# Hybrid GLA/NSA/SSD decoder trunk: the mixers' small TensorE products regrouped by array tile shape

## The chip, the core and the metric

The kernel runs on one core of one Trainium2 chip. The metric is the device time of one execution in microseconds, as the median of several runs. [...] In what follows the tile shape is written rows x columns, so 64x128 is half of the rows and all columns.

## The reference

Two layers on 256 tokens of 1,024 features, float32. In each layer an RMSNorm and one input projection feed three token mixers. Their outputs are concatenated, projected and added to the residual, and an MLP with squared ReLU follows.

```python
for l in range(DEPTH):
    u = rms_norm(h, norm1_w[l])
    proj = u @ w_in[l]
    ...
    y_gla = gla_mixer(...)
    y_nsa = nsa_mixer(...)
    y_ssd = ssd_mixer(...)
    h = h + jnp.concatenate([y_gla, y_nsa, y_ssd], axis=-1) @ w_out[l]
    u = rms_norm(h, norm2_w[l])
    h = h + jnp.square(jax.nn.relu(u @ w_up[l])) @ w_down[l]
return rms_norm(h, final_norm_w)
```

- **GLA** (gated linear attention, 4 heads of 32 keys and 64 values): a gate of rank 16 gives a log decay per key, summed along the tokens (B). Attention between tokens i and j is weighted by exp(B_i - B_j).
- **NSA** (sparse attention, 4 heads of 64, two per key/value group g): each query attends to 15 compressed keys, to selected blocks and to a window, with a softmax for each of the three branches; with 256 tokens the selected blocks and the window are all earlier tokens. The compressed keys and values come from a small MLP (2,048 to 128 to 64) over blocks of 32 tokens.
- **SSD** (Mamba-2, 8 heads of 64, state 128): a causal convolution, a cumulative decay per head, chunked scan in two chunks of 128 tokens, gated norm.

## The kernel before

Tokens are two halves t of 128. Weights come in pieces of 512 KB: `load_w` (L172) issues the DMA on SyncE's queue into one of three raw buffers, `split_w` (L181) makes a high part (a cast, mostly on ScalarE, L100) and a low part (a subtraction on VectorE, L189) in five buffers each, and a matrix product is then three TensorE passes (`mm3`, L262, and L428 to L430). So the large products are float32r of shape 128x128. The mixers' small products are plain float32, each of which appears as two TensorE instructions, and transposes.

The work of a layer's first part is written as five generators (L400 to L988): `s_proj` (13 units of 256 columns of the input projection, order in `CFG['porder']`), `s_nsa`, `s_gla`, `s_ssd` and `s_out`. `drive` (L272) steps the one whose own clock is lowest, each `yield` being a cost, and so sets the order in which instructions are written; the scheduler of the framework then places each ready instruction by that order. Engines execute in the order that comes out of this at build time. While a mixer waits for VectorE or ScalarE, TensorE thus has projection matmuls to do. Small products write to a pool of four PSUM banks (`psb`, L107), projections to another four (`psa`).

The small products that matter here, with the tile shape that they use:

- `s_gla`: transposes of the gate's 16 columns (L797), the gate product with 16 rows (L800: 32x128). Then three levels of block products. Level 0 (L881) has stationary operands of 32, 64 and 96 columns; levels 1 and 2 (L899) are 32x32-token blocks, 24 products of 32 columns for each level and token half (128x32), and the diagonal products (L923) eight more for each half. Each level's factors (VectorE, ScalarE) are written just ahead of its products, the diagonal ones after level 2. The output product `goT` (L936 128x128 for t=1, L939 128x64) is written for t=0 before the diagonal products of t=1.
- `s_ssd`: five products for the cumulative decays `aps` (L664 to L667), three of them with 8 or 16 stationary columns, alternating with two of 128; two DMAs (L673, L674) move the negated sums to four partitions, and a copy and a subtraction make `acs_st` (L680, L681).
- `s_nsa`: the second product of the compression MLP (L518 with 64 columns per group, L521 with 15). For each token half and each head (r, g) `score` (L550) writes a mask into a bank by a bf16 product with the identity (L557, 128x128), adds the scores by a product with 64 rows (L560 for t=0; L563, L565 for t=1: 64x128, g choosing the lower or the upper half of the rows), for t=1 adds a second mask (L566, 128x128), and then takes three maxima (VectorE, L569) and three exponentials (ScalarE, L571). `trans` (L574) transposes the probabilities, and `value` (L594) multiplies: one product with the 15 compressed values (L601: 15 rows, 32x128) and two or four of 128 rows (L604). `NSEQ` (L29) is the order of these steps.

```python
PE.matmul(sa[:, :271], lhsT=identb, rhs=mask_t1 if t else mask_t0, start=True, stop=False)
...
PE.matmul(sa[:, :271], lhsT=q1, rhs=kT[gs, 0:271], start=False, stop=True)
sb = psb(f"sb{l}{t}{hh}")
PE.matmul(sb[:, :256], lhsT=q1, rhs=kT[gs, 271:527], start=True, stop=False)
PE.matmul(sb[:, 128:256], lhsT=identb, rhs=mask_cau, start=False, stop=True)
```

The compression MLP's first weights (`w1`, L498) use the same three raw buffers as the projection's weights, and hold two of them until its products (L501) have run.

Of the kernel before, what the change touches and what calls it, by code (L numbers as in the profile page):

```python
# [7 lines left out]
F32 = mybir.dt.float32  # L8
# [20 lines left out]
NSEQ = ([("s", 0, 0), ("s", 0, 1), ("t", 0, 0), ("s", 1, 0), ("t", 0, 1), ("s", 1, 1), ("v", 0), ("t", 1, 0), ("t", 1, 1), ("v", 1)],  # L29
        [("s", 0, 0), ("s", 0, 1), ("t", 0, 0), ("s", 1, 0), ("t", 0, 1), ("s", 1, 1), ("c",), ("t", 1, 0), ("v", 0),  # L30
# [16 lines left out]
for _n, _w in (("ident", 128), ("tri", 128), ("sfx", 128), ("ones64", 128), ("sel", 128), ("hmask", 4),  # L47
               ("sel4", 30), ("cosk", 128), ("sink", 128), ("cosq", 128), ("sinq", 128), ("valid", 2), ("e", 8), ("ta", 2)):
    _cf(_n, _w)
# [3 lines left out]
for _n, _w in (("n1", 8), ("n2", 8), ("gb", 1), ("gn", 2), ("nn", 2), ("cw", 32), ("cb", 8), ("sn", 4),  # L53
               ("pos", 32), ("w2", 128), ("dtb", 8), ("alog", 8), ("dsk", 8)):
    PF[_n] = (PF_N, PF_N + _w)
    PF_N += _w
# [3 lines left out]
def trunk(ctx, tc, x, w_in, w_out, w_up, w_down, w1, par, gate2, fnw, constf, constb, consti, out):  # L60
# [22 lines left out]
    rp = ctx.enter_context(tc.tile_pool(name="rp", bufs=2))  # L83
# [31 lines left out]
    with prio(-20000):  # L115
# [3 lines left out]
        for l in range(L):  # L119
            p = mpool.tile([128, PF_N], F32, name=f"par{l}", tag="par", bufs=2)  # L120
            g2 = mpool.tile([16, 128], F32, name=f"g2_{l}", tag="g2", bufs=2)
            pars.append(p)
            gates2.append(g2)
# [6 lines left out]
    with prio(5):  # L130
# [3 lines left out]
        SP.dma_start(gates2[0], gate2[0])  # L134
# [7 lines left out]
    mask_t1 = cb[:, 399:670]  # L142
    mask_ssd = cb[:, 670:798]
    mask_cau = cb[:, 128:256]
    hmask = C("hmask")
    sel = C("sel").rearrange("p (r m) -> p r m", r=2)
    cosk, sink, cosq, sinq = (C(n).rearrange("p (t d) -> p t d", t=2) for n in ("cosk", "sink", "cosq", "sinq"))
# [3 lines left out]
    onesc = cpool.tile([128, 128], F32, name="onesc")  # L151
    V.memset(onesc, 1.0)
    with prio(-30000):
        wps = psb("warm")
        for _ in range(CFG["warm"]):
            PE.matmul(wps[:, 0:128], lhsT=onesc, rhs=onesc, start=True, stop=True)
# [13 lines left out]
    G.memset(zt, 0.0)  # L170

# [125 lines left out]
    for l in range(L):  # L297
        p, g2 = pars[l], gates2[l]
        if l:
            SP.dma_start(p, par[l])  # L300
            SP.dma_start(g2, gate2[l])
# [19 lines left out]
        misc = mpool.tile([128, 2, 36], F32, name=f"misc{l}", tag="misc")  # L321
# [27 lines left out]
        def ev1(t, ps):  # L349
            rope(q_r[:, t], ps, 4, cosq, sinq, t, f"q{l}{t}")  # L350
# [103 lines left out]
        def s_nsa():  # L454
            w2 = P_["w2"].rearrange("p (v d) -> p v d", v=2)
# [8 lines left out]
            cp("qT", qT, qps.rearrange("p (r t) -> p r t", r=2), "A")  # L464
# [25 lines left out]
            gl = mpool.tile([128, 2, 30], F32, name=f"gl{l}", tag="gl")  # L490
            vc = mpool.tile([15, 128], F32, name=f"vc{l}", tag="vc")

            def comp(kv):
# [21 lines left out]
                V.tensor_tensor(gl[:, kv], t1, xx, OP.mult)  # L515
                for g in range(2):
                    if kv == 0:
                        PE.matmul(cps[g * 64:g * 64 + 64, 320:335], lhsT=w2[:, 0], rhs=gl[:, 0, g * 15:g * 15 + 15],  # L518
                                  start=True, stop=True)
                    else:  # L520
                        PE.matmul(cps[0:15, 336 + g * 64:400 + g * 64], lhsT=gl[:, 1, g * 15:g * 15 + 15], rhs=w2[:, 1],  # L521
                                  start=True, stop=True)
                if kv == 0:
                    A.copy(kT[:, 256:271], cps[:, 320:335])
                else:
                    A.copy(vc, cps[0:15, 336:464])
# [16 lines left out]
            br = (1, 0, 2)  # L543
            for t in range(2):
                segs = [(0, 128), (128, 143), (143, 271)] if t == 0 else [(0, 256), (256, 271), (271, 527)]
                sm = [spool.tile([128, 2, 3], F32, name=f"sm{l}{t}{r}", tag="sm", bufs=4) for r in range(2)]
                prs, pts, pcs = {}, {}, []
                yn = n2(f"yn{l}{t}", [128, 2, 128])

                def score(r, g):  # L550
                    gs = slice(g * 64, g * 64 + 64)
                    hh = 2 * g + r
                    pr = prp.tile([128, 527], F32, name=f"pr{l}{t}{hh}", tag="pr")
                    prs[r, g] = pr
                    q1 = qT[gs, r, t * 128:t * 128 + 128]
                    sa = psb(f"sa{l}{t}{hh}")
                    PE.matmul(sa[:, :271], lhsT=identb, rhs=mask_t1 if t else mask_t0, start=True, stop=False)  # L557
                    nm = spool.tile([128, 3], F32, name=f"nm{l}{t}{hh}", tag="nm", bufs=4)
                    if t == 0:
                        PE.matmul(sa[:, :271], lhsT=q1, rhs=kT[gs, 128:399], start=False, stop=True)  # L560
                        src = [sa[:, a:b] for a, b in segs]
                    else:
                        PE.matmul(sa[:, :271], lhsT=q1, rhs=kT[gs, 0:271], start=False, stop=True)  # L563
                        sb = psb(f"sb{l}{t}{hh}")
                        PE.matmul(sb[:, :256], lhsT=q1, rhs=kT[gs, 271:527], start=True, stop=False)  # L565
                        PE.matmul(sb[:, 128:256], lhsT=identb, rhs=mask_cau, start=False, stop=True)  # L566
                        src = [sa[:, 0:256], sa[:, 256:271], sb[:, 0:256]]
                    for i in range(3):
# [626 lines left out]
```

## Time and profile before

| | us |
|---|---|
| median of 3 runs | 699.27 (699.01 to 699.5) |
| the profiled execution, first to last instruction | 698.9 |
| TensorE busy | 678.2 |
| VectorE busy | 473.7 |
| ScalarE busy | 367.7 |
| mixers and projections of layer 0, of layer 1 | about 10 to 172, 350 to 510 |
| MLP of layer 0, of layer 1 | about 172 to 349, 510 to 686 |

A row of the timeline view has the start of the first instruction of a run of equal ones, the time until the last of them ends, the engine, line, operation, output and inputs, the stationary operand's shape (rows*columns), the moving one's, and how many there are. [...] A row of the windows view has, for one stretch, its length, then each engine's busy time and instructions, the granted TensorE clock as a share, the busy share of the DMA engines and GB/s.

### The profile page before, as it was taken

The page shows a single profiled execution, that of the slowest core. Times are in us where ns is not written, and L with a number is a line of the kernel's source. Part 1 is how long each engine was busy: PE and PEld are TensorE (multiplying, and loading weights), DVE is VectorE, ACT ScalarE, POOL GpSimd, SP SyncE. Part 2 cuts the span into 40 slices and gives each one's busy share as a digit, 9 for nine tenths or more (in the row PEclk, how much of TensorE's full clock was granted, in tenths as well). Part 3 has the DMA queues.
Part 4 walks back from the last instruction along what each step waited for, and adds up shares of the span by engine and source line. Part 5 has one row for each costly group of instructions (what it writes and reads, how often), then busy time and mean ns, then how long its engine had stood idle before and what let it go on. Part 6 is the DMA issues. An engine that isn't in the chain of part 4 may idle for free.

```text
span 698.9 us, 12400 instructions
## 1 busy us (share of the span) xinstructions
PE 678.2 (97%) x4926; PEld 607.8 (87%) x4926; DVE 473.7 (68%) x880; ACT 367.7 (53%) x704; POOL 5.5 (1%) x16
## 2 busy tenths in 40 slices
PE   4999999999999999999999999999999999999996
PEld 4987888987999898989898889798889999999995
DVE  5885886988755555554579878788886555555535
ACT  7344856656644444454364376764575444444433
POOL 2000000000000000000000000000000000000000
PEclk9998999999999999999999999999999999999999
DMA  8524741433765555556414374332466655555521
GB/s 276 188 80 154 225 121 58 121 117 126 238 212 187 188 191 188 181 182 187 153 61 152 113 235 142 96 119 84 129 205 213 207 183 187 189 192 184 181 91 60
DMA packets 31873, 111.81 MB, mean 160 GB/s; under 512 B 3688, under 2 KB 4296, under 8 KB 31816
## 3 DMA queue, kind: packets, MB, share of 16 engines
q1 hardware_dynamic: 31816, 111.04, 49.2%
q8 instruction: 38, 0.62, 0.3%
q14 instruction: 19, 0.16, 0.1%
HBM read 109.94 MB, written 1.05 MB: 159 GB/s over the span
## 4 chain that ended last, share of the span: by engine, by line
PE 90%; DMA 4%; DVE 3%; ACT 2%; issue 0%; SPq 0%; DVEq 0%; ACTq 0%
PE acc L263 8%; PE up L264 8%; PE up L265 8%; PE up L263 8%; PE acc L265 8%; PE acc L264 8%; DMA r_in<-in_w_in 4%; PE pj L263 3%; PE pj L265 3%; PE pj L264 3%; PE pj L428 3%; PE pj L429 3%; PE pj L430 3%; PE op L265 2%; PE op L263 2%; PE op L264 2%
## 5 line engine op out<-in xcount | busy, mean ns | idle before, releaser
L265 PE MATMUL up<-xh_b,l_u 128*128 128x256 f32 x480 | 135.7, 283 | 0.0
L264 PE MATMUL up<-xl_b,h_u 128*128 128x256 f32 x480 | 135.7, 283 | 0.0
L263 PE MATMUL up<-xh_b,h_u 128*128 128x256 f32 x480 | 135.7, 283 | 0.0
L189 DVE TENSOR_TENSOR l_d<-r_d,h_d 128x1024 fp32r<-128x1024 f32 x64 | 78.4, 1225 | 70.2 <-ACT h_d L100 69.9
L189 DVE TENSOR_TENSOR l_u<-r_u,h_u 128x1024 fp32r<-128x1024 f32 x64 | 78.2, 1224 | 69.1 <-ACT h_u L100 69.0
L100 ACT CAST h_u<-r_u 128x1024 fp32r<-128x1024 f32 x64 | 67.1, 1049 | 82.8 <-PE up L264 40.1
L100 ACT CAST h_d<-r_d 128x1024 fp32r<-128x1024 f32 x64 | 67.0, 1048 | 80.3 <-PE up L264 43.7
L265 PE MATMUL acc<-h_d,ul 128*128 128x512 f32 (+1 forms) x288 | 106.7, 370 | 0.0
L264 PE MATMUL acc<-l_d,uh 128*128 128x512 f32 (+1 forms) x288 | 106.3, 369 | 0.0
L263 PE MATMUL acc<-h_d,uh 128*128 128x512 f32 (+1 forms) x288 | 106.2, 369 | 0.0
L264 PEld LDWEIGHTS up<-xl_b,h_u 128*128 128x128 f32 x480 | 91.9, 191 | 0.6
L263 PEld LDWEIGHTS up<-xh_b,h_u 128*128 128x128 f32 x480 | 91.8, 191 | 0.6
L265 PEld LDWEIGHTS up<-xh_b,l_u 128*128 128x128 f32 x480 | 91.9, 192 | 0.0
L189 DVE TENSOR_TENSOR l_in<-r_in,h_in 128x1024 fp32r<-128x1024 f32 (+2 forms) x54 | 64.3, 1194 | 20.1 <-ACT h_in L100 19.7
L100 ACT CAST h_in<-r_in 128x1024 fp32r<-128x1024 f32 (+2 forms) x50 | 50.9, 1021 | 36.9 <-PE pj L265 10.6
L263 PE MATMUL pj<-h_in,xh_a 128*128 128x256 f32 (+1 forms) x224 | 66.2, 296 | 0.0
L265 PE MATMUL pj<-h_in,xl_a 128*128 128x256 f32 (+1 forms) x224 | 65.8, 295 | 0.0
L264 PE MATMUL pj<-l_in,xh_a 128*128 128x256 f32 (+1 forms) x224 | 65.0, 291 | 0.0
L263 PEld LDWEIGHTS acc<-h_d,uh 128*128 128x128 f32 x288 | 54.3, 189 | 9.8 <-ACT uh L231 0.8
L265 PEld LDWEIGHTS acc<-h_d,ul 128*128 128x128 f32 x288 | 54.1, 188 | 10.0 <-DVE ul L232 0.4
L264 PEld LDWEIGHTS acc<-l_d,uh 128*128 128x128 f32 x288 | 54.1, 188 | 9.4
L428 PE MATMUL pj<-xh_a,h_in 128*128 128x256 f32 x192 | 57.2, 298 | 2.0 <-ACT h_in L100 2.0
(347 smaller groups left out, 1244.7 us busy)
## 6 DMA issues: line engine op xcount, KB each, us to landing
r_u<-in_w_up SPq DMA_DIRECT2D x64, 512.0 KB, 3.3
r_d<-in_w_down SPq DMA_DIRECT2D x64, 512.0 KB, 3.3
r_in<-in_w_in SPq DMA_DIRECT2D x48, 512.0 KB, 4.3
r_o<-in_w_out SPq DMA_DIRECT2D x16, 512.0 KB, 3.5
r_w<-in_w SPq DMA_DIRECT2D x8, 512.0 KB, 4.3
r_in<-in_w_in SPq DMA_DIRECT2D x4, 438.0 KB, 3.7
out_dram<-o SPq DMA_DIRECT2D x4, 256.0 KB, 2.0
r_in<-in_w_in SPq DMA_DIRECT2D x2, 292.0 KB, 3.9
```

Source lines behind the costliest of these rows:

```text
L100: A.copy(dst, src)
L189: i_ = V.tensor_tensor(lo[:, :n], raw[:, :n], hi[:, :n].bitcast(F32), OP.subtract)
L263: PE.matmul(ps, lhsT=lh, rhs=rh, start=start, stop=False)
L264: PE.matmul(ps, lhsT=lh, rhs=rl, start=False, stop=False)
L265: PE.matmul(ps, lhsT=ll, rhs=rh, start=False, stop=stop)
L428: PE.matmul(o, lhsT=wh[:, ts], rhs=xh[:, k], start=k == 0, stop=False)
L429: PE.matmul(o, lhsT=wh[:, ts], rhs=xl[:, k], start=False, stop=False)
L430: PE.matmul(o, lhsT=wl[:, ts], rhs=xh[:, k], start=False, stop=k == 7)
```

## The change

No large product changes. The mixers' small products do:

- **Scores in pairs.** `score(r, part)` now does both groups g at once: two masks first (128x128), then the product of g=0 on the lower row half and that of g=1 on the upper, into two PSUM banks, then the maxima and exponentials of both. For t=1 the two parts of the row are separate steps; the second part's mask is now 256 columns wide and stands first. A scheduling order (`behind`) keeps the products behind both masks. `NSEQ` has the new order.
- **Padding with zeros to 128x128.** The 15 compressed values and probabilities (`vc`, `pc`, `pt`), the gate's operands (`misc`, `g2`, `glT`), the decay increments (`dap`: one product of 128 columns gives the sums of both halves on partitions 0 to 7 and 32 to 39, in place of three narrow ones), the compression's second product (`glp`, `w2` with its key half twice) and GLA's level 0. The padded tiles are cleared by GpSimd once at the start.
- **GLA levels in a row.** The factors of levels 1 and 2 and of the diagonal are written one after the other; then, for each token half, all small products of levels 1, 2 and the diagonal follow each other, and then their copies. Both `goT` come after that, with the 128x128 products ahead of the 128x64 ones.
- **What follows from these:** four DMAs in place of two for the negated sums, two copies and two subtractions for `acs_st`, the copy of the compressed keys in two parts (ScalarE and VectorE), the query scale of 1/8 in the copy of `qT` instead of in two tables (256 constant columns fewer), one rope buffer in place of two.

```diff
-NSEQ = ([("s", 0, 0), ("s", 0, 1), ("t", 0, 0), ("s", 1, 0), ("t", 0, 1), ("s", 1, 1), ("v", 0), ("t", 1, 0), ("t", 1, 1), ("v", 1)],
-        [("s", 0, 0), ("s", 0, 1), ("t", 0, 0), ("s", 1, 0), ("t", 0, 1), ("s", 1, 1), ("c",), ("t", 1, 0), ("v", 0),
+NSEQ = ([("s", 0, 0), ("s", 1, 0), ("t", 0, 0), ("t", 0, 1), ("v", 0), ("t", 1, 0), ("t", 1, 1), ("v", 1)],
+        [("s", 0, 0), ("s", 0, 1), ("s", 1, 0), ("t", 0, 0), ("s", 1, 1), ("t", 0, 1), ("c",), ("t", 1, 0), ("v", 0),
...
+                    for g in range(2):
+                        mk = mask_w1 if part else mask_t1 if t else mask_t0
+                        i_m = PE.matmul(sc[g][:, 0:n], lhsT=identb, rhs=mk, start=True, stop=False)
+                    for g in range(2):
+                        i_s = PE.matmul(sc[g][:, 0:n], lhsT=q1[g], rhs=kT[g * 64:g * 64 + 64, k0:k0 + n], start=False, stop=True)
+                        if g == 0:
+                            behind(i_s, i_m)
...
-                        pcx = pt[0:15, 256:384] if t == 0 else pcs[0][:, (r * 2 + g) * 128:(r * 2 + g) * 128 + 128]
+                        pcx = pt[:, 256:384] if t == 0 else pcs[0][:, (r * 2 + g) * 128:(r * 2 + g) * 128 + 128]
...
-            for t in range(2):
-                if t:
-                    PE.matmul(aps[:, 8:16], lhsT=C("tri"), rhs=da[:, t], start=True, stop=True)
-                PE.matmul(aps[0:8, 128 + t * 128:256 + t * 128], lhsT=da[:, t], rhs=C("tri"), start=True, stop=True)
+            PE.matmul(aps[:, 8:16], lhsT=C("tri"), rhs=da[:, 1], start=True, stop=True)
             PE.matmul(aps[:, 16:24], lhsT=C("sfx"), rhs=da[:, 0], start=True, stop=True)
-            PE.matmul(aps[0:16, 384:512], lhsT=da.rearrange("p t h -> p (t h)"), rhs=C("tri"), start=True, stop=True)
+            PE.matmul(aps[:, 128:256], lhsT=dap.rearrange("p a b -> p (a b)"), rhs=C("tri"), start=True, stop=True)
...
-            SP.dma_start(nst[0:2], nah.bitcast(F32))
-            SP.dma_start(nst[2:4], nal.bitcast(F32))
+            for t in range(2):
+                SP.dma_start(nst[t:t + 1], nah[32 * t:32 * t + 8].bitcast(F32))
+                SP.dma_start(nst[2 + t:3 + t], nal[32 * t:32 * t + 8].bitcast(F32))
...
+            factors(0)
+            yield 3.0
+            for t in range(2):
+                ps = psb(f"gl{l}{t}0")
+                for a in (1, 2, 3):
+                    PE.matmul(ps[:, (a - 1) * 128:a * 128].rearrange("p (h s) -> p h s", h=4),
+                              lhsT=kv_lv[0][:, a - 1, t * 128:t * 128 + 128],
+                              rhs=qls[0].rearrange("p h (n a s) -> p h n a s", n=2, a=3)[:, :, t, a - 1],
+                              start=True, stop=True)
...
+            factors(1)
+            yield 3.0
+            factors(2)
...
+            for t in range(2):
+                gp = psb(f"gl{l}{t}x")
+                for i in (1, 2):
...
+                            PE.matmul(gp[32 * b:32 * b + 32, o:o + 32].rearrange("p (h n s) -> p h n s", h=4, n=w),
+                                      lhsT=kv_lv[i][:, a - 1, t * 128 + 32 * b:t * 128 + 32 * b + 32], rhs=rhs,
+                                      start=True, stop=True)
                 for z in range(2):
                     for b in range(4):
                         c0 = t * 128 + 32 * b
-                        PE.matmul(gps[t][32 * b:32 * b + 32, 192 + z * 64:256 + z * 64].rearrange("p (h n) -> p h n", h=4),
+                        PE.matmul(gp[32 * b:32 * b + 32, 192 + z * 64:256 + z * 64].rearrange("p (h n) -> p h n", h=4),
                                   lhsT=(k4 if z else ks)[:, c0:c0 + 32], rhs=qbd[:, :, c0 + z:c0 + 32:2],
                                   start=True, stop=True)
...
+                if t == 1:
+                    for pr_ in range(2):
+                        PE.matmul(goT[:, pr_ * 128:pr_ * 128 + 128], lhsT=gst[:, pr_ * 128:pr_ * 128 + 128], rhs=qx,
+                                  start=pr_ == 0, stop=False)
+                for hh in range(4):
+                    z, pr_ = hh % 2, hh // 2
+                    PE.matmul(goT[z * 64:z * 64 + 64, pr_ * 128:pr_ * 128 + 128], lhsT=gv[:, t, hh * 64:hh * 64 + 64],
+                              rhs=at[:, hh], start=t == 0, stop=t == 0 or hh >= 2)
```

More of the change, by code (lines that the diff above doesn't have):

```diff
@@ L150, in trunk @@
     mask4 = ci[:, 24:56].rearrange("p (z n) -> p z n", z=2)
-    onesc = cpool.tile([128, 128], F32, name="onesc")
+    onesc = cpool.tile([128, 1], F32, name="onesc")
     V.memset(onesc, 1.0)
[L153 to L156, printed above, removed]
     er = cpool.tile([68, 8, 128], FR, name="er")
@@ L514, in comp @@
                 V.reciprocal(t1, t1)
[L515 to L518, printed above, removed]
-                                  start=True, stop=True)
[L520 to L526, printed above, removed]
+                V.tensor_tensor(gl[:, kv * 30:kv * 30 + 30], t1, xx, OP.mult)
+                if kv == 0:
+                    PE.matmul(cps[:, 320:350], lhsT=w2[:, 0:128], rhs=gl[:, 0:30], start=True, stop=True)
+                    A.copy(kT[0:64, 256:271], cps[0:64, 320:335])
+                    V.tensor_copy(kT[64:128, 256:271], cps[64:128, 335:350])
+                else:
+                    for g in range(2):
+                        PE.matmul(cps[:, 352 + g * 64:416 + g * 64], lhsT=gl[:, 30 + g * 15:g * 15 + 158], rhs=w2[:, 128:192],
+                                  start=True, stop=True)
+                    A.copy(vc[0:15], cps[0:15, 352:480])
                 yield 2.0
@@ L542, in s_nsa @@
                 yield None
-            br = (1, 0, 2)
             for t in range(2):
-                segs = [(0, 128), (128, 143), (143, 271)] if t == 0 else [(0, 256), (256, 271), (271, 527)]
                 sm = [spool.tile([128, 2, 3], F32, name=f"sm{l}{t}{r}", tag="sm", bufs=4) for r in range(2)]
-                prs, pts, pcs = {}, {}, []
+                prs, nms, pts, pcs = {}, {}, {}, []
                 yn = n2(f"yn{l}{t}", [128, 2, 128])
[L550 to L561, printed above, removed]
-                    else:
[L563 to L568, printed above, removed]
-                        V.tensor_reduce(nm[:, br[i]:br[i] + 1], src[i], AX.X, OP.max, negate=True)
-                    for i, (a, b) in enumerate(segs):
-                        A.activation(pr[:, a:b], src[i], AF.Exp, bias=nm[:, br[i]:br[i] + 1],
-                                     accum_out=sm[r][:, g, br[i]:br[i] + 1])
@@ L679, in s_ssd @@
             A.activation(edc, aps[:, 16:24], AF.Exp)
-            A.copy(acs_st[0:8, :], aps[0:8, 128:384])
-            V.tensor_tensor(acs_st[32:40, :], aps[0:8, 128:384], acs_st[0:8, :].bitcast(F32), OP.subtract)
             yield 1.0
```

200 lines of the change are left out of this document (106 added, 94 removed).

## The prediction

> **What bounds the kernel now.** I read the page first, for who is busy and who holds the end.
>
> ```profile
> span 698.9 us, 12400 instructions
> PE 678.2 (97%) x4926; PEld 607.8 (87%) x4926; DVE 473.7 (68%) x880; ACT 367.7 (53%) x704; POOL 5.5 (1%) x16
> PE 90%; DMA 4%; DVE 3%; ACT 2%; issue 0%; SPq 0%; DVEq 0%; ACTq 0%
> ```
>
> TensorE is busy nearly all the time and is 90% of the chain that ended last. So a microsecond of TensorE's time counts, unless it lies in one of the few stretches in which TensorE waits for another. "Busy" here also holds what a product loses at its borders, and that shows in the timeline of TensorE: look at the distance of the starts, not at the durations.
>
> ```profile
> 32.55 0.28 PE L428 MATMUL pj<-xh_a,h_in 128*128 128x256 f32 x1
> 32.67 0.28 PE L429 MATMUL pj<-xl_a,h_in 128*128 128x256 f32 x1
> ...
> 34.47 0.38 PE L430 MATMUL pj<-xh_a,l_in 128*128 128x256 f32 x1
> 34.70 0.28 PE L428 MATMUL pj<-xh_a,h_in 128*128 128x256 f32 x1
> ```
>
> ```profile
> 137.63 1.00 PE L749 MATMUL yp<-xdt,mt 128*128 128x64 f32 x8
> 138.47 0.38 PE L738 MATMUL seg<-cb 128*128 128x512 bf16 x1
> ```
>
> Projection matmuls follow each other every 0.12 us (32.55, 32.67), each with its own weights; small float32 products of the full shape every 0.105 (0.84 for eight). But after the ten `aps` instructions of changing shape the first projection matmul takes 0.23 until the next starts (34.47, 34.70). The rule that I read from this and from the rows below: when the tile shape changes, the instruction ahead of the border costs about 0.09 us more, since the array has to run empty, and the first one behind it some 0.10 more, since the next weights can't be loaded under it (less for fewer stationary columns). A border thus costs up to 0.19 us, and the change is about borders.
>
> **Part 1: values (L601 padded from 15 to 128 rows).**
>
> ```profile
> 86.26 0.28 PE L557 MATMUL sa<-cb 128*128 128x271 bf16 x1
> 86.47 0.72 PE L560 MATMUL sa<-kT,qT 64*128 64x271 f32 x2
> 87.12 0.43 PE L601 MATMUL no<-vc,pt 15*128 15x64 f32 x2
> 87.48 0.66 PE L604 MATMUL no<-vsw,pt 128*128 128x64 f32 x4
> 88.06 0.43 PE L601 MATMUL no<-vc,pt 15*128 15x64 f32 x2
> ```
>
> ```profile
> L601 PE MATMUL no<-vc,pt 15*128 15x64 f32 x16 | 3.4, 294 | 0.0
> L601 PE MATMUL no<-vc,pc 15*128 15x64 f32 x16 | 3.4, 294 | 0.0
> ```
>
> From 87.12 to 88.06 six instructions take 0.94 us; without borders six take 0.66 at 0.11. That is 0.28 a product. The 32 instructions in the two groups are 16 products, 8 in a layer: 2.24 us per layer. The padding adds nothing on TensorE, since 64 moving columns on a full set of weights cost the 0.11 anyway; the copy of `pc` has as many elements per partition as before.
>
> **Part 2: scores in pairs.** For t=0 mask and score take 0.86 us (86.26 to 87.12), and the follower pays 0.10: 0.96, four times, 3.84 us. A pair afterwards: mask 0.12, mask ahead of the border 0.21 (86.26 to 86.47), first product 0.33, last 0.32 (the 0.65 from 86.47 to 87.12), 0.10 behind: 1.08 us, if the two row halves work at the same time. If they work one after the other, two more instructions of 0.23 (0.32 less the 0.09): 1.54. Two pairs: saved 1.68, or 0.76. For t=1:
>
> ```profile
> 101.11 0.28 PE L557 MATMUL sa<-cb 128*128 128x271 bf16 x1
> ...
> 102.48 0.28 PE L557 MATMUL sa<-cb 128*128 128x271 bf16 x1
> ```
>
> 1.37 us each, four times 5.48. Afterwards each r has two pairs, 1.08 and about 1.04 with 256 in place of 271 columns: 4.24 for two r, saved 1.24; one after the other 6.1, so 0.6 lost. The row halves at the same time are not in this trace. The nearest rows are column tiles:
>
> ```profile
> 49.14 1.11 PE L501 MATMUL cps<-r_w,zt 128*32 128x128 f32 x32
> 50.07 0.33 PE L899 MATMUL gl00x<-ql,klv 128*32 128x32 f32 x18
> ```
>
> 32 instructions in 0.93 us: eight rounds of about 0.11, each with four column tiles at once. I take the row halves as doing the same: 2.92 us per layer, with 0.2 as the other end. [...] No run here shows it yet.
>
> **Part 3: decays, gate, level 0.** `aps`: 2.03 us from 32.67 to 34.70. Afterwards three products, six instructions at 0.11, between two projection matmuls of 0.12: 0.90. Saved 1.13.
>
> ```profile
> 30.26 0.28 PE L428 MATMUL pj<-xh_a,h_in 128*128 128x256 f32 x1
> ...
> 31.37 0.28 PE L430 MATMUL pj<-xh_a,l_in 128*128 128x256 f32 x1
> ```
>
> ```profile
> 40.52 0.28 PE L264 MATMUL pj<-l_in,xh_a 128*128 128x256 f32 x1
> 40.73 2.25 PE L881 MATMUL gl<-ql,klv 128*32 128x128 f32 x12
> ...
> 42.93 0.28 PE L263 MATMUL pj<-h_in,xh_a 128*128 128x256 f32 x1
> ```
>
> The gate product with its neighbours takes 1.11; without borders two projection matmuls (0.24) and two of 256 columns (0.44): saved 0.43. Level 0: 2.41 from 40.52 to 42.93; afterwards 12 x 0.11 and two of 0.12, 1.56: saved 0.85. Together 2.4 us per layer. But they stand in a stretch where VectorE is nearly full:
>
> ```profile
> 27.00:44.00 17.00, 17.00 (x126) 14.49 (x125) 15.45 (x45) 8.71 (x29) 0.00 (x0) 1.00 0.42 138
> 50.30:57.40 7.10, 5.54 (x139) 4.60 (x125) 4.67 (x27) 2.76 (x8) 0.00 (x0) 0.99 0.49 150
> 57.40:64.10 6.70, 6.69 (x58) 5.48 (x59) 3.37 (x11) 0.95 (x3) 0.00 (x0) 0.50 0.51 168
> 81.00:117.00 36.00, 35.90 (x255) 30.63 (x255) 28.13 (x71) 25.71 (x76) 0.00 (x0) 1.00 0.40 126
> ```
>
> ```profile
> 50.31 5.98 DMA r_in<-in_w_in
> ...
> 57.41 0.58 PE pj L428
> ```
>
> VectorE has 15.45 of 17.00 us, so what TensorE leaves earlier it can reach only by the 1.55 it is idle. And the next thing that must come is the compression MLP: its products free the raw buffers, the next weights start at 50.31 and TensorE uses them at 57.41. In 50.30 to 57.40 TensorE is busy 5.54 of 7.10 us: there it waits for weights. So of the 2.4 I count 0.9 (some of VectorE's idle 1.55), between 0 and 2.4.
>
> **Part 4: GLA levels in a row, compression, output product.** Levels 1, 2 and the diagonal visit the 32-column shape in eight groups per layer, afterwards in two. A visit costs 0.09 into it, 0.03 for the short weights, 0.09 and 0.10 out of it, 0.31; several share a border with a neighbour, so six fewer are 1.2 to 1.9 us. The compression's second products save about 0.3, `goT` two borders, 0.2 to 0.4. But most of this stands in the stretch that waits for weights: what it frees becomes waiting. I count 0.2 for `goT` of t=1 and 0.5 because groups that come after the weights now can move into the hole: 0.7, between 0 and 2.6.
>
> **What is added.**
>
> ```profile
> 34.87 0.78 SPq L673 DMA_DIRECT2D nst<-nac  x1
> ```
>
> ```profile
> 37.07 0.41 DVE L681 TENSOR_TENSOR acs_st<-aps,acs_st 8x256 fp32r<-8x256 f32 x1
> ```
>
> Two more DMAs of about 0.78 on SyncE's queue; behind them the next weight load, which waits for a subtraction until about then. Its piece is used over ten microseconds later, so zero, at worst 1.6 us, where that reserve is gone. One more VectorE copy, subtraction and ScalarE copy each, below 0.41: up to 0.8 us per layer on VectorE, which I take out of the 0.9 already. The memsets are on GpSimd (5.5 us busy in all) at the start. One rope buffer costs nothing, as VectorE writes and reads it in order.
>
> **The sum.** Per layer 2.24 + 2.92 + 0.9 + 0.7 = 6.76 us, two layers 13.5. The profiled execution is 698.9 us, 0.4 below the median of 699.27. 698.9 - 13.5 = 685.4, and with the 0.4, rounded, 686.0. Parts 1 and 2 lie mostly behind 81 us, where TensorE is busy 35.90 of 36.00 us with projections as filler. VectorE has 28.13 of these 36.00; if TensorE needs 5 us less, VectorE is 91% full: it still fits, but with little room.
>
> **The rivals.** Three runs spread over 0.5 us, and about 0.2%, 1.4 us, is what a measurement can tell from no change.
>
> *Row halves one after the other.* Parts 1, 3 and 4 stay, part 2 gives 0.2 in place of 2.92: 5.4 us less in two layers, 691.4. For it: no row shows row halves together. Against: the column tiles are.
>
> *The freed time comes back as waiting.* VectorE at 91% and an order fixed at build time leave TensorE behind maxima and exponentials. If half of the sum is lost: 692.7.
>
> *The clock drops in layer 1 too.* In 57.40 to 64.10 the granted clock is 0.50, right behind the stretch in which TensorE waited for weights; the same stretch of layer 1 has no drop. Less work in these stretches may give a drop in both. At half clock 6.7 us of work lose up to 3.35: 689.3. [...]
>
> *Nothing is hidden.* Parts 3 and 4 whole: 2.24 + 2.92 + 2.4 + 2.2 = 9.8 per layer, 19.5 in all: 679.8; without the drop in layer 0 676.4.
>
> *Slower: the pairs hold the PSUM pool.* A pair takes two of the four banks and gives them back only after its maxima and exponentials, so two pairs hold all; whatever small product is next in TensorE's order then waits, and the projections behind it.
>
> ```profile
> L569 DVE TENSOR_REDUCE nm<-sa x40: 160/279/426, 78.9 to 447.6; 128x1 f32<-128x128 f32 x16, 128x1 f32<-128x15 f32 x16, 128x1 f32<-128x256 f32 x8
> L571 ACT ACTIVATE pr<-sa,nm x40: 255/361/479, 80.6 to 448.3; 128x128 f32<-128x128 f32 x16, 128x15 f32<-128x15 f32 x16, 128x256 f32<-128x256 f32 x8
> ```
>
> Forty and another eight for the second part are 24 exponentials in a layer; 24 maxima and exponentials of 0.28 + 0.36 are 15.4 us per layer if TensorE stands for all of them. It decides from 6.76 us on, 44% of that. At the full price 686.0 + 30.8 = 716.8. Against: projections fill TensorE there now, and before the change t=1 took two banks for each head as well.
>
> *The change does nothing*, since the time saved lies where something else is late: within 1.4 us of 699.27.
>
> **How the numbers follow.** Forecast (686.0, own range 683 to 689) 0.46; clock drop in layer 1 0.15; halves in sequence 0.11; half comes back 0.10; nothing hidden 0.11; slower 0.04; nothing 0.03. Faster is the sum of the first five, 0.93; same 0.03, slower 0.04. The range goes from 679, just below the case in which nothing is hidden, to 693, just above the case in which half comes back; left out are the drop that vanishes as well, the slower case and what lies between, together below 0.2.
>
> **What would show it.** In the timeline after: values and `aps` at about 0.11 us per instruction with no 0.20 between; a pair's four score instructions starting two and two, a few nanoseconds apart, 0.65 from the first to the follower (if 1.1, the halves run in sequence); the stretch like 50.30 to 57.40 still 6 to 7 us long with more waiting in it; granted clock 0.50 in one stretch, not two; VectorE above 85% in the stretch like 81 to 117. Wrong it is if the borders keep their 0.09 and 0.10 after padding, if TensorE waits for maxima and exponentials, or if part 3 shows in full before 44 us.

## The result: slower by 1.2%, and the profile after

The changed kernel takes 708.44 us (median of 4 runs, 705.41 to 709.98), the kernel before 699.38 (4 runs): a ratio of 1.012, with a 95% interval of 1.0101 to 1.0139. The forecast was 686.0, with a range of 679 to 693. It was wrong on the side to which 0.04 had been given. The profiled execution after is the one of 705.41 us.

First its page: the span, the busy times, and the chain of work that ended last.

```profile
span 703.6 us, 12394 instructions
...
PE 669.1 (95%) x4914; PEld 604.2 (86%) x4914; DVE 472.5 (67%) x884; ACT 369.2 (52%) x706; POOL 6.3 (1%) x22
...
PE 75%; DVE 10%; DMA 9%; ACT 5%; issue 1%; SPq 0%; ACTq 0%; DVEq 0%
```

TensorE is busy 9.1 us less than before (669.1 for 678.2), and yet the span is 4.7 us longer. TensorE's part of the chain fell from 90% to 75%; VectorE, ScalarE and the DMAs took its place. So the borders did go, and waiting came for more than they had cost: leaving out the transposes of the norms (`nt_a`, `nt_b`), the view of waits lists 15.9 us of TensorE's waits after and 3.8 before.

The granted clock tells the other half. It is 0.979 to 0.988 in the four executions after (the profiled one has the highest), and 0.991 to 0.999 in the 25 of the kernel before that were run beside the first experiments. A stretch at half clock enters this mean with half its length (in the profile after, 13.65 us at 0.50 and 3.9 more at the span's end, out of 703.6, give 0.988), so TensorE loses at most (1 - clock) of the span by it: projection matmuls follow each other every 0.21 us in these stretches and every 0.12 outside (medians of 13 and of 1,115). That is an estimate of up to 12.2 us on average after and 2.8 before. The difference, 9.4, is as large as the whole loss of 9.1. So the waits can cost most of this through the stretches at half clock that follow them.

The padded products themselves run as forecast. This is the timeline of TensorE after; the first number is the start. Rows overlap: before, the projection matmul of 32.55 has 0.28 us, and the next starts at 32.67. So a time is read from start to start.

```profile
88.93 0.33 PE L609 MATMUL no<-vc,pt 128*128 128x64 f32 x2
89.10 0.61 PE L612 MATMUL no<-vsw,pt 128*128 128x64 f32 x4
89.54 0.28 PE L587 MATMUL tp<-cf,pr 128*128 128x128 f32 x1
```

```profile
109.02 0.37 PE L565 MATMUL sb<-cb 128*128 128x256 bf16 x1
109.32 0.70 PE L567 MATMUL sb<-kT,qT 64*128 64x256 f32 x4
109.95 0.66 PE L587 MATMUL tp<-cf,pr 128*128 128x128 f32 x4
```

```profile
33.95 0.28 PE L435 MATMUL pj<-xl_a,h_in 128*128 128x256 f32 x1
34.12 0.39 PE L671 MATMUL aps<-dap,cf 128*128 128x8 f32 x2
...
34.81 0.36 PE L436 MATMUL pj<-xh_a,l_in 128*128 128x256 f32 x1
35.01 0.28 PE L434 MATMUL pj<-xh_a,h_in 128*128 128x256 f32 x1
```

Six value instructions take 0.61 us (88.93 to 89.54) where they took 0.94. The four score instructions of a pair take 0.63 (109.32 to 109.95), where one head after the other would need about 1.1; they start two and two, the second of each two 7 ns behind the first by the trace. The decays with their neighbours take 1.06 (33.95 to 35.01) where they took 2.03.

Now the waits of TensorE: who it waited for, in all, how often, and the longest.

```profile
PE tp L587 <- ACT pr L579: 4.4, 4, 1.3
PE sa L565 <- ACT pr L579: 4.4, 4, 1.8
...
PE zps L485 <- ACT kwv L100: 1.3, 2, 0.7
PE kps L537 <- DVE cm L934: 1.2, 2, 0.6
```

```profile
PE tp L579 <- ACT pr L571: 0.9, 2, 0.5
```

Before, in the second block, waits for exponentials were 0.9 us in all; they are 8.8 now, and there are two waits that were not there: for the copy of `kwv` (L100), and for a PSUM bank that VectorE frees when it has read the GLA row (`cm`, L934). Both stand ahead of the second half of the compression MLP. In layer 1 the chain of waits of the changed kernel goes through that place:

```profile
390.60 6.51 DMA r_in<-in_w_in
...
397.13 1.04 ACT h_in L100
398.18 0.20 ACT at L100
...
399.32 0.27 ACT kwv L100
...
399.64 0.69 PE zps L485 x8
...
407.18 0.65 PE cps L506 x16
...
407.85 3.67 DMA r_in<-in_w_in
...
411.54 1.05 ACT h_in L100
```

Read it upwards. The weights at 411.54 are late because their DMA began at 407.85. It could begin only when the compression products (L506) had read a raw buffer that held their own weights, at 407.18 to 407.83. These products waited for the selection (L485), which waited for `kwv`, and the copy of `kwv` stood on ScalarE behind a cast of weights (which had waited for its DMA until 397.13) and behind four copies of `cm` to `at`. Here is ScalarE's timeline, after and then before:

```profile
397.13 1.04 ACT L100 CAST h_in<-r_in 128x1024 fp32r<-128x1024 f32 x1 [2.69 <-DMA r_in<-in_w_in]
398.08 1.21 ACT L100 COPY at<-cm 32x128 f32<-32x128 f32 x4
399.32 0.27 ACT L100 COPY kwv<-pj 128x128 f32<-128x128 f32 x1
399.68 1.22 ACT L100 COPY at<-cm 32x128 f32<-32x128 f32 x4
400.92 0.27 ACT L100 COPY kwv<-pj 128x128 f32<-128x128 f32 x1
```

```profile
395.42 0.27 ACT L100 COPY kwv<-pj 128x128 f32<-128x128 f32 x1
396.50 0.27 ACT L100 COPY kwv<-pj 128x128 f32<-128x128 f32 x1 [0.81 <-DVE rp_w L342]
397.18 1.04 ACT L100 CAST h_in<-r_in 128x1024 fp32r<-128x1024 f32 x1 [0.41 <-DMA r_in<-in_w_in]
```

Before, both copies of `kwv` ran ahead of that cast, and the copies of `cm` came 5 us behind it. The last sixteen of the second compression products were then done by 401.46:

```profile
400.86 0.60 PE cps L501 x16
```

After, the last of them end at 408.22, 6.8 us later. The same 6.8 us of layer 1 look like this, before and then after (busy time of TensorE, its weight loads, VectorE, ScalarE and GpSimd, the granted clock, the DMA share and GB/s):

```profile
399.30:406.10 6.80, 6.54 (x80) 5.45 (x76) 4.73 (x18) 4.38 (x12) 0.00 (x0) 1.00 0.66 235
```

```profile
395.90:399.32 3.42, 1.04 (x5) 0.67 (x5) 1.75 (x7) 2.13 (x5) 0.00 (x0) 1.00 0.02 4
399.30:406.10 6.80, 6.46 (x37) 4.71 (x38) 2.15 (x11) 2.47 (x8) 0.00 (x0) 0.50 0.27 80
```

The DMA queue moved 235 GB/s there and moves 80 now. After, TensorE works for 1.04 us out of 3.42, and then 6.8 us at half clock, with 37 instructions where there were 80. The same happens behind the scores at 105.77 and at 450.52, for 3.4 us each.

### The profile page after: what moved, and what is told of

Same layout as the page of the kernel before. It is cut to its first block, busy times and chain, and to the rows that moved or that the text cites. A ratio compares the mean times of both kernels' runs of the same rounds, so it can differ in the third digit from the quotient of the medians.

```text
span 703.6 us, 12394 instructions
## 1 busy us (share of the span) xinstructions
PE 669.1 (95%) x4914; PEld 604.2 (86%) x4914; DVE 472.5 (67%) x884; ACT 369.2 (52%) x706; POOL 6.3 (1%) x22
## 4 chain that ended last, share of the span: by engine, by line
PE 75%; DVE 10%; DMA 9%; ACT 5%; issue 1%; SPq 0%; ACTq 0%; DVEq 0%
PE up L271 8%; PE up L270 8%; PE up L272 8%; PE acc L270 8%; PE acc L271 8%; PE acc L272 8%; DMA r_in<-in_w_in 7%; PE pj L272 3%; PE pj L270 3%; PE pj L271 2%; ACT h_in L100 2%; DVE l_in L196 2%; PE pj L435 2%; PE pj L434 2%; PE pj L436 2%; PE no L612 2%
## 5 line engine op out<-in xcount | busy, mean ns | idle before, releaser
L100 ACT CAST h_u<-r_u 128x1024 fp32r<-128x1024 f32 x64 | 67.1, 1048 | 86.7 <-DMA r_u<-in_w_up 46.5
L100 ACT CAST h_d<-r_d 128x1024 fp32r<-128x1024 f32 x64 | 67.1, 1048 | 75.3 <-PE up L271 41.8
L100 ACT CAST h_in<-r_in 128x1024 fp32r<-128x1024 f32 (+2 forms) x50 | 50.8, 1023 | 44.0 <-DMA r_in<-in_w_in 19.2
L271 PE MATMUL pj<-l_in,xh_a 128*128 128x256 f32 (+1 forms) x224 | 66.6, 299 | 0.0
```

Of the source, the lines that this page charges most:

```text
L100: A.copy(dst, src)
L271: PE.matmul(ps, lhsT=lh, rhs=rl, start=False, stop=False)
```

## The experiments

Two theories stood at the start. **O, the order:** the GLA row, emitted early, puts its copies on ScalarE and its products on TensorE ahead of the second half of the compression. **P, the pairs:** a pair asks for six exponentials at once, and TensorE waits for them. A third, **S**, was that the load of the norm weights, wider because `w2` comes with them, delays the start: the first transposes stand at 8.69 us after, at 6.83 before. Every time below is beside runs of the kernel before on the same chip; a ratio is to those.

**e1 and e2: each part undone.** e1 puts the GLA levels back (the loop of before, with the padded level 0), e2 the scores.

```diff
-            factors(1)
-            yield 3.0
-            factors(2)
...
-            for t in range(2):
-                gp = psb(f"gl{l}{t}x")
-                for i in (1, 2):
...
+            for i, (Pp, Ss) in enumerate(((128, 32), (32, 8), (8, 2))):
...
+                yield 3.0
+                if i == 0:
...
+                else:
+                    if i == 1:
+                        gps = [psb(f"gl{l}{t}x") for t in range(2)]
```

> The changed kernel with the GLA levels and diagonal back in the order of before (each level's products behind its own factors); padding, pairs of scores and the new output product stay. Theory O (order): the GLA row puts eight copies of cm to at on ScalarE ahead of the two copies of kwv, so that the second half of the compression MLP, its weights and the next projection come late, 6.3 us in layer 1 and about 2 in layer 0. Then this kernel gets that back: 698 to 701 us, and the clock keeps 1.0 in the stretch 399 to 406. Theory P (pairs): the pairs of scores make TensorE wait for exponentials in t=0; they are still here, so 705 to 709. Theory S (start): the wider load of the norm weights costs 1.8 at the start and is still here: at least 1.8 more than the border sum, with either.

Measured: 699.11 us, ratio 0.9985 (0.9958 to 1.0011). As O has it: undoing the row takes the whole loss away. It does not bring the gain that the borders promised.

```diff
-NSEQ = ([("s", 0, 0), ("s", 1, 0), ("t", 0, 0), ("t", 0, 1), ("v", 0), ("t", 1, 0), ("t", 1, 1), ("v", 1)],
+NSEQ = ([("s", 0, 0), ("s", 0, 1), ("t", 0, 0), ("s", 1, 0), ("t", 0, 1), ("s", 1, 1), ("v", 0), ("t", 1, 0), ("t", 1, 1), ("v", 1)],
...
-                def score(r, part):
+                def score(r, g):
```

> The changed kernel with the scores one head at a time, as before (mask, score, mask, score); padding and the GLA row stay. Theory O: the compression comes as late as in the changed kernel: 705 to 711 us (the pairs' own saving of borders is lost as well). Theory P: the waits of TensorE for exponentials are gone, 698 to 701.

Measured: 708.51 us, ratio 1.0115 (1.0073 to 1.0158). Taking out the pairs alone gives nothing back, against P alone. The waits for exponentials are gone in it (0.4 us in all), but TensorE now waits 6.0 us for VectorE's convolution at L387: where one wait goes, the next is close behind.

**e3: both undone.** Only the padding and the new output product are left.

> The changed kernel with both undone: only the padded products and the output product in its new order are left. By the prediction's terms for values, early padding and output product (2.24 + 0.9 + 0.2 in each of two layers, 6.7 us): 692.6; with theory S 1.8 more, 694.4. If O and P both hold and add up, this is the fastest of the four, 692 to 695. If it stays at 699 or above, the padding itself brings nothing.

Measured: 701.57 us, ratio 1.0002 (0.9973 to 1.0032). This was the surprise: the padding, 6.7 us by the prediction's terms, brings nothing. In its profile the clock is at one half for 6.8 us in layer 0 (as in that of before) and for another 6.8 us in layer 1. Over its ten executions the granted clock is 0.990 on average, where before has 0.996: up to 4.3 us of the 6.7 can have gone there, by the estimate above. S fell with these kernels: with the wide load in all of e1 to e4, the first transposes stand at 6.76 to 6.91 us. So the late start after is most likely that execution's own, and 1.8 of the 4.7 us between the two profiles not the change's.

**e4: the row stays, but later.** One number in the changed kernel:

```diff
             cp("k4", k4[:, 1::2], ks[:, 1::2], "V")
-            yield 3.0
+            yield 6.0
```

> The changed kernel with one number changed: the stream that emits the GLA row gives way to the others for 6.0 units of its cost in place of 3.0 ahead of the row, so that the copies of kwv and of the keys stand ahead of the copies of cm on ScalarE; the row itself, the pairs and the padding stay. Theory O: 696 to 700 us, at least as fast as with the old GLA order, since the row's saved borders stay. If it is the row as such that costs (its PSUM banks, its burst of work on VectorE), and not its place: 704 to 709. Theory P: 705 to 709.

Measured: 694.91 us, ratio 0.9927 (0.9903 to 0.9950). Nothing is computed otherwise than in the changed kernel, and it is 13.5 us faster; its granted clock is 0.995 on average, so that up to 8.5 us of these are less time at half clock. ScalarE's timeline and the chain of waits in layer 1:

```profile
390.89 0.27 ACT L100 COPY kwv<-pj 128x128 f32<-128x128 f32 x1 [0.61 <-DVE rp_w L348]
392.16 1.05 ACT L100 CAST h_in<-r_in 128x1024 fp32r<-128x1024 f32 x1 [1.00 <-DMA r_in<-in_w_in]
393.12 0.26 ACT L100 COPY kwv<-pj 128x128 f32<-128x128 f32 x1
...
396.00 0.61 ACT L100 COPY at<-cm 32x128 f32<-32x128 f32 x2 [2.35 <-DVE cm L938]
```

```profile
395.60 0.56 PE cps L506 x14
...
396.18 4.52 DMA r_in<-in_w_in
```

The copies of `kwv` are ahead of those of `cm` again, the second compression products end at 396.54 (after: 408.22; layer 1 itself begins 3.9 us sooner here), and the next weights follow at once.

**e5: e4 with single scores.** The edit of e2 on e4.

> The row of e4 (started later) with the scores one head at a time, as before: what the pairs are worth when the order around the compression is in place. By the prediction's term the pairs bring 2.92 us in each layer, so this kernel should be 5.8 us slower than e4's 694.9: about 700.7. With the old GLA order they brought 2.5 (699.1 against 701.6) and with the row early nothing (708.4 against 708.5). If what they save turns into waiting wherever the order is fixed before the run, 695 to 698.

Measured: 697.38 us, ratio 0.9962 (0.9938 to 0.9986). The pairs bring 2.5 us, as between e1 and e3, not the 5.8 of the prediction; the intervals of e4 and e5 overlap, and so do those of e1 and e3, so the 2.5 rests on the two agreeing. All waits of TensorE but those of the norms' transposes add up to 10.1 us in e4 and 6.8 in e5: the 3.3 that are missing from 5.8. Here are the waits ahead of the transposes of the probabilities and of `cbp` in e4, then those ahead of the transposes in e5:

```profile
PE tp L587 <- ACT pr L579: 3.0, 2, 1.8
PE cbp L722 <- DVE xa L389: 2.5, 2, 1.3
```

```profile
PE tp L583 <- ACT pr L575: 0.8, 1, 0.8
```

**e6 and e9: the values alone.** e6 is the kernel before with `vc`, `pc` and the transposes behind `pc` padded.

```diff
-            vc = mpool.tile([15, 128], F32, name=f"vc{l}", tag="vc")
+    vc = cpool.tile([128, 128], F32, name="vc")
+    G.memset(vc, 0.0)
...
-                            PE.transpose(tq[0:15, (r * 2 + g) * 128:(r * 2 + g) * 128 + 128], prs[r, g][:, 256:271], ident)
-                    pc = n2(f"pc{l}{t}", [15, 512])
+                            PE.transpose(tq[:, (r * 2 + g) * 128:(r * 2 + g) * 128 + 128], prs[r, g][:, 256:384], ident)
+                    pc = n2(f"pc{l}{t}")
...
-                        pcx = pt[0:15, 256:384] if t == 0 else pcs[0][:, (r * 2 + g) * 128:(r * 2 + g) * 128 + 128]
+                        pcx = pt[:, 256:384] if t == 0 else pcs[0][:, (r * 2 + g) * 128:(r * 2 + g) * 128 + 128]
```

> The kernel before with the padded values alone (15 rows to 128, and the copy of pc with them). TensorE's, ScalarE's and SyncE's instructions stand in the same order as before, so nothing moves but the borders: by the prediction's term 2.24 us in each layer, 4.5 in all: 0.9936 of the kernel before. If the saved time comes back as waiting even in the same order: within 0.3% of before.

Measured: 699.46 us, ratio 0.9996 (0.9969 to 1.0023): no gain. But the expectation said something untrue. The order is not that of before: TensorE's list differs from the wider transposes on (layer 0, 111 us), presumably because these count for more in the planner's costs. In layer 1 the products of the state-space part, `cbp`, begin at 469.80 (before: 468.56), although the transposes ahead of them end 4.7 us sooner. e9 therefore keeps the transposes at 15 rows and clears the buffer on GpSimd; its lists for TensorE, VectorE, ScalarE and SyncE are those of before, row by row. The rest of its edit is that of e6.

```diff
-                    pc = n2(f"pc{l}{t}", [15, 512])
-                    cp("pc", pc, tq[0:15, :], "A")
+                    pc = n2(f"pc{l}{t}")
+                    G.memset(pc, 0.0)
+                    cp("pc", pc[0:15], tq[0:15, :], "A")
```

> The kernel before with the values' products alone padded to 128 rows, and this time really nothing moved: the transposes and the copy of pc keep their 15 rows (GpSimd clears the buffer of pc ahead, once in a layer), so that TensorE, VectorE, ScalarE and SyncE have the same instructions in the same order as before; e6 also widened those transposes, and with them part of TensorE's order moved behind the second half of the scores, against what its expectation said. If the border saving reaches the end when the order stays: 4.5 us less, 0.9936 of before. If it comes back as waiting in any case: within 0.2% of before, and e6's new order is not what ate it.

Measured: 695.78 us, ratio 0.9932 (0.9910 to 0.9955); forecast 0.9936. TensorE's timeline in e9:

```profile
87.66 0.39 PE L603 MATMUL no<-vc,pt 128*128 128x64 f32 x2
87.88 0.61 PE L606 MATMUL no<-vsw,pt 128*128 128x64 f32 x4
88.33 0.50 PE L580 MATMUL tp<-cf,pr 128*128 128x128 f32 x3
```

Six instructions take 0.67 us, 0.27 less for each product (forecast 0.28). The saving reaches the end when nothing else moves: 4.7 us between the medians (700.52 and 695.78), at the same mean granted clock of 0.996, where 4.5 were forecast and the interval leaves 3.2 to 6.3. e6 has a mean clock of 0.994, the kernel before beside it 0.997: up to 2.0 of the 4.5 us that it lacks are time at half clock.

**e7: the order alone.** The kernel before with every product as it was; only the GLA stream is hurried.

```diff
-                yield 3.0
+                yield {0: 3.0}.get(i, 0.0)
                 if i == 0:
```

> The kernel before, with no product changed; only the stream that emits the GLA levels no longer gives way behind the factors of levels 1 and 2 (0 in place of 3.0 units), so that the copies of cm on ScalarE stand ahead of the copies of kwv, as in the changed kernel. Theory O (order): this alone makes the kernel before slower by about what the changed kernel lost, 8 to 14 us: 707 to 713. If the row or the padding were needed for the loss: 698 to 702.

Measured: 713.69 us, ratio 1.0170 (1.0123 to 1.0217). The loss of the changed kernel, and more, without any of its products. ScalarE in layer 1 has the pattern of after, and the compression follows late, 45.1 us behind the last transposes of the layer's first norm (before 39.9, after 47.2):

```profile
405.58 1.04 ACT L100 CAST h_in<-r_in 128x1024 fp32r<-128x1024 f32 x1 [2.01 <-DMA r_in<-in_w_in]
406.54 1.22 ACT L100 COPY at<-cm 32x128 f32<-32x128 f32 x4
407.77 0.43 ACT L100 COPY kwv<-pj 128x128 f32<-128x128 f32 x2
```

```profile
412.75 0.65 PE cps L501 x16
...
413.42 3.57 DMA r_in<-in_w_in
```

**e8: the copies on another engine.** In the changed kernel:

```diff
-                    cp("atb", ats[t][bs, :, bs], cmps[t][bs], "A")
+                    cp("atb", ats[t][bs, :, bs], cmps[t][bs], "V")
```

> The changed kernel with the eight copies of cm to at moved from ScalarE to VectorE; the row stays in its early place in TensorE's order. If it is ScalarE's queue that holds kwv back (the copies of cm ahead of it): 697 to 702. If it is the place of the row in TensorE's order and the PSUM bank that the keys wait for, which VectorE frees: 705 to 711, since VectorE now has the copies as well.

Measured: 697.64 us, ratio 0.9964 (0.9937 to 0.9990). With the row in its early place in TensorE's list, but its copies off ScalarE, the loss is gone. Why is less tidy. The compression is still late:

```profile
402.73 1.04 PE cps L506 x32
```

Counted from the last transposes of the layer's first norm, its second products end at 44.9 us in layer 1 (after 47.2) and at 45.3 in layer 0 (after 43.0): as late as in e7, which loses 14 us. So a late compression alone is not the loss, whatever the chain above suggests. What did go are the waits for exponentials, from 8.8 us to 0.8, and the granted clock is 0.992 on average, up from 0.983. So the copies most likely hurt through ScalarE. The run does not show through which of the instructions behind them, and the planner sorted the other instructions anew here too.

**e10 and e11: more of the same.** e10 is e4 and e8 together, e11 is e4 with 8.0 in place of 6.0.

> e4 (row later) and e8 (copies of cm on VectorE) together. Each alone brought the changed kernel from 708 to 695 and to 698. If both mend the same wait, as theory O has it, together they give no more than the better one: 693 to 697. If they mend different waits, up to another 5 us: 688 to 692.

> e4 with the row later still, 8.0 units in place of 6.0. If the early place of the row is all that hurt, this does not differ from e4 by more than its scatter: 693 to 697. If every place of the row has its own price by what it collides with, it can lie anywhere from 690 to 703.

Measured: e10 693.52 us, ratio 0.9903 (0.9869 to 0.9937); e11 696.29, ratio 0.9938 (0.9920 to 0.9956). Both intervals overlap that of e4. This fits e8 and e4 mending the same wait, and it says that 8.0 units do as well as 6.0; other places were not tried.

**e12 and e14: the exponentials first.** e12 on e4, e14 on the changed kernel with the row early:

```diff
-                        for i, (a, b) in enumerate(runs):
-                            o = 0 if part == 0 else 271
...
+                        with tc.high_priority():
+                            for i, (a, b) in enumerate(runs):
+                                o = 0 if part == 0 else 271
```

> e4 with the exponentials of the scores ahead of whatever else ScalarE's planned order has ready. Theory P, in what is left of it: in e4 TensorE waits 3.0 us for exponentials ahead of the transposes of the weights (0.8 in e5, without pairs), since a pair asks for six of them at once and they stand between casts of weights. With the exponentials first that wait should be below 1 us and the time 2 us less, 692 to 694. If the casts that are pushed back make the projections wait in its place: 695 or more.

Measured: e12 692.01 us, ratio 0.9875 (0.9837 to 0.9913). The time is what P expected, the reason is not: the wait ahead of the transposes stays at 2.6 us. What went is the wait of `cbp` for VectorE (2.5 in e4). Against e4 the intervals overlap, so the gain of 2.9 us is possible and not shown.

> The changed kernel with the exponentials first on ScalarE and the row in its early place. If the waits for exponentials (8.8 us of TensorE in t=0) are a loss of their own: 701 to 705. If they only follow from the compression that comes late: 706 to 710, with the waits moved elsewhere.

Measured: e14 703.64 us, ratio 1.0062 (1.0041 to 1.0082), where the changed kernel has 1.012 with an interval that does not meet it. So the exponentials behind casts of weights are a loss of their own, about 4 us of the 9. The waits of the scores (`sa`, 4.4 us) are gone, those of the transposes stay at 4.3. Of the half-clock stretches at 105, 399 and 450 us none is left, while one of 6.83 us is back at 57.96, as before; the granted clock is 0.992 on average, so the 4 us can be half-clock time alone (up to 6.3 us less of it than after).

**e13: all three mends.**

> The changed kernel with the row later (6.0), the copies of cm on VectorE and the exponentials first: e10 and e12 together. If the mends are of different waits: e12's 692.0 less e10's gain over e4 of 1.4: 690 to 691. If VectorE, fuller by the copies, is the next bound: 693 or more.

Measured: 692.04 us, ratio 0.9885 (0.9858 to 0.9911). No more than e12, and between the two expectations. These two are the fastest found, 1.2% below the kernel before, with all products of the change in them.

## Why the prediction was wrong, step by step

A table of the two stretches that the change touches, from the start of the last transpose of a layer's first norm to that of its second norm, in us:

| kernel | layer 0 | of it at half clock | layer 1 | of it at half clock |
|---|---|---|---|---|
| before | 151.75 | 6.83 | 148.62 | 0 |
| after | 150.04 | 3.41 | 154.49 | 10.24 |
| e9, values alone, same order | 149.92 | 3.41 | 146.41 | 0 |
| e4, row later | 147.34 | 3.41 | 147.60 | 0 |
| e7, before with the GLA hurried | 159.10 | 13.65 | 154.84 | 3.41 |
| e12, e4 with the exponentials first | 145.89 | 3.41 | 146.89 | 6.83 |

Half of a time at half clock is at most what TensorE lost by it. In layer 1, after is 5.87 us longer than before, and up to 5.1 of them are that.

- **Part 1, values, 2.24 a layer: right.** e9 gives 2.21 in layer 1, where neither profile has a drop of the clock. In layer 0 it gives 1.83, but up to 1.7 of these are the shorter stretch at half clock; what carries the term is the 4.7 us between the medians of whole executions.
- **Part 2, pairs, 2.92 a layer: the local cost was right, its effect not.** The halves do run at the same time (0.63 us for four, forecast 0.65 with 271 columns). But 5.8 us forecast became 2.5 (e4 against e5, e1 against e3), since TensorE now stands in other waits, for exponentials above all. That it would wait for them was among the prediction's own signs of being wrong. The rival "the freed time comes back as waiting" described this, for the sum as a whole; it holds for this term. The bank-holding rival was on the right trail too: the new wait of `sa` for exponentials is a wait for a bank that they still read.
- **Part 3, decays, gate, level 0, 0.9 of 2.4: about right.** The first compression products begin at 389.50 us in layer 1 (390.58 before), of which 0.5 was gained ahead of the layer; 0.6 remains. That VectorE would hide the rest fits: after, it is busy 17.68 of the 18.50 us from 27.00 on.
- **Part 4, GLA row, 0.7: here it failed.** The step was "0.5 because groups that come after the weights now can move into the hole". It moved TensorE's groups and counted nothing else that moves with them: eight copies on ScalarE and the reads of the row on VectorE. The list of what is queued behind them was never made. Behind them stood `kwv`, and behind `kwv` the raw buffers, and later the exponentials. In place of 0.5 us of gain stand 13.5 us between the row early and the row late (after against e4), and 10.8 with the copies alone taken off ScalarE (e8).
- **The added work on SyncE's queue and VectorE at nothing: no sign against it.** The early part came out ahead in spite of it.
- **The rival "the clock drops in layer 1 too" came true,** with one further place in each layer, while the drop at 57.24 that it started from is gone after. Ahead of each of its stretches in the profile after, TensorE was busy for 1.04 to 1.40 us out of 3.41; that waiting brings them is the author's estimate from these three. In the two profiles the stretches within the span are 13.65 us long after and 6.83 before, up to 3.4 us more, about the 3.35 that it was given; over all executions it is up to 9.4, and there the rival was priced too low.
- **The border rule itself counted too much behind the border.** Where a projection matmul follows small float32 products or transposes of the full shape, it takes 0.20 us until the next starts (median of 38 places in the trace of before), and 0.22 behind a change of shape (29 places). So of the 0.10 that the rule gives to the first instruction behind a border, 0.08 stays after padding when that is a projection. The sums of part 3 have this in them. Of the reasons that the rule names, the weight loads in the trace of before show one: in a row of full shapes a load starts 0.12 ahead of its product (median of 4,170; 32.44 for 32.55), behind a border 2 ns ahead of it (median of 164; 86.46 for 86.47). As to the array running empty, the trace shows that a product behind a border starts 0.07 ahead of the recorded end of the one before it, and 0.16 in a row of full shapes (medians of the same); the rest is the author's reading.
- **The sum:** all terms were priced on the order of before. The order of every engine's list is worked out anew from the planner's costs when any instruction changes. e7 shows that this alone moves the time by 14 us, as much as the whole forecast of 13.5; e6 shows it eating a saving of 4.5 us that e9 has in full. The range of 679 to 693 had no room for such a cause, and none of the rivals was it. The 0.2% that the prediction allowed for telling a change was narrow as well: the executions of the kernel before lie between 696.67 and 705.01 us.

What stays open: how much of e8's gain comes through `kwv` and how much through the exponentials behind; why e7 loses 14 us with a compression no later than that of e8; and by what e12 gains over e4, if it does. Of these runs e9 alone is shown to keep the order of TensorE, VectorE, ScalarE and SyncE; in e4, e6, e7, e8 and e14 the planner moved more than the edit names.

## What to carry to other kernels

When a group of products is moved on TensorE, list what else it carries along (its copies on ScalarE, its reads on VectorE, its PSUM bank), and find on each of these engines the instruction that will now stand behind: price the move by who waits for that one. Where a planner fixes the order, first compare the lists of all engines before and after, and measure a saving with the lists held the same (e9) before believing or dropping it. An engine whose casts wait for DMAs was a bad place here for short copies with something urgent behind them: one word that sends them to another engine (e8), or one number that lets their stream start later (e4), was worth 10.8 and 13.5 us, where the forecast had counted 13.5 for the whole change and its seventy-eight borders (154 before, 76 after, those of the transposes of 15 and 16 columns not counted). And read the granted clock of all executions beside the times: in the profile after, waits of about 2 us within 3.41 were followed by 3.41 or 6.83 us at half clock, which can cost as much again (by the estimate above up to 1.7 or 3.4).

## What the runs showed of the hardware

- **TensorE was partly busy ahead of the half-clock stretches.** Those of all kernels that end within the span are 3.41, 6.83 or 10.24 us long. Ahead of each one after, TensorE was busy part of the time only, as in the first row here; the second is the half-clock stretch itself:

```profile
102.36:105.77 3.41, 1.21 (x8) 0.49 (x6) 3.41 (x10) 1.73 (x9) 0.00 (x0) 1.00 0.74 238
105.77:109.18 3.41, 3.41 (x15) 2.47 (x14) 1.94 (x8) 2.16 (x12) 0.00 (x0) 0.50 0.13 44
```

  1.21 us of 3.41 here, 1.04 of 3.42 ahead of 399.32, 1.40 ahead of 450.52. What decides is not shown by these runs, and the busy time alone does not: the 3.41 us ahead of the drop at 57.24 before were busy for 2.21, while 1.63 out of the 3.41 from 163.93 on in e10 had no drop behind them:

```profile
163.93:167.34 3.41, 1.63 (x11) 1.14 (x11) 3.39 (x6) 3.17 (x7) 0.00 (x0) 1.00 0.52 136
```

- **Behind float32 products and transposes of the full shape the first projection cost some 0.08 us more.** In the timeline of the decays the first projection matmul behind them takes 0.20 until the next starts (34.81 to 35.01), as in the median of the 38 places of before; behind another projection the median is 0.12. The prediction had put this into the border; it is half of why the decays took 1.06 us and not 0.90.
- **Parts of the array worked at once, by their starts.** In the compression products of before (128x32, from 49.14 on) four start 5 to 7 ns apart and the next four 0.11 us behind; in the score pairs after (64x128, from 109.32 on) two start 7 ns apart and the next two 0.32 behind.
